# Order of the input projections beside the differential attention of a two-layer hybrid encoder

## The chip, the cores and the metric

The kernel runs on one core of a Trainium2 chip. The metric is the device time of one execution in microseconds (us), the median of several runs. The core's engines work side by side, each through its own instructions in a fixed order: PE (TensorE: matmuls and transposes), DVE (VectorE), ACT (ScalarE), POOL (GpSimd) and SP (SyncE, which here issues nearly all transfers). An instruction that has to wait holds up everything behind it on its engine.

## The reference

Two layers work on 2048 tokens of width 1024. Each projects the normalized input to 3584 columns, which four groups of heads share: A (dense attention with normalized queries and keys), B (a window of 128 to each side), C (a two-dimensional neighbourhood with a bias table), and D (differential attention: two softmaxes of all keys, one subtracted from the other). Each group's output is multiplied by its gate, then comes an output projection and the residual. The core, cut:

```python
for l in range(DEPTH):
    h = _rmsnorm(x, norm_g[l])
    z = jnp.einsum('bsd,de->bse', h, w_in[l])
    (q_a, k_a, v_a, g_a, q_b, k_b, v_b, g_b,
     q_c, k_c, v_c, g_c, q_d, k_d, v_d, g_d) = jnp.split(z, offs, axis=-1)
    q_a = _axial_rope(_rmsnorm(q_a.reshape(...), qn_a[l]), row, col)
    k_a = _axial_rope(_rmsnorm(k_a.reshape(...), kn_a[l]), row, col)
    o_a = _dense_blocked(q_a, k_a, v_a, sc_hd)
    q_b, k_b = _rope(q_b, t), _rope(k_b, t)
    o_b = _window_sink(q_b, k_b, v_b, sink_b[l], sc_hd)
    o_c = _neighbourhood(q_c, k_c, v_c, rpb_c[l], sc_hd)
    q_d, k_d = _rope(q_d, t), _rope(k_d, t)
    o_d = _diff_blocked(q_d, k_d, v_d, lam, DIFF_DIM ** -0.5)
    o_d = _rmsnorm(o_d, subln_d[l]) * (1.0 - lam_init)
    mix = jnp.concatenate([o_a * silu(g_a), o_b * silu(g_b), o_c * silu(g_c), o_d * silu(g_d)], -1)
    x = x + jnp.einsum('bsm,md->bsd', mix, w_out[l])
return _rmsnorm(x, final_g)
```

## The kernel before

The 2048 tokens are 16 tiles of 128. A layer has four stages. First the columns of D are projected for all tiles. Then comes the D phase: D's attention, in 32 units (one tile and one group of keys each), and beside it, as filler for PE, the projections of A, B and C. Then the attention of A, B and C, and last the output projection.

A unit of D makes scores on PE (S, L497, 16 of 128 x 512), takes them from PSUM with their maxima on DVE (L498), exponentiates on ACT (L505), subtracts the second softmax from the first on DVE (L724), transposes on PE (PTp, L514), copies back on ACT (L475), multiplies with the values on PE (O, L521), and finishes with a norm: DVE's L594, L595 and L597, POOL's L114 and L545, and PE's transpose L550 (fin).

The filler is a generator (`filler`) that `drive` advances by some steps at each slot of D's work. It works through `plan`: ten chunks of 256 columns for tiles 0 to 7, then the same ten for tiles 8 to 15. A tile of a chunk is 24 matmuls (z, L320, L322, L324: two parts of the input, two of the weight, eight blocks of rows), and then the chunk's post-processing:

- `q_chunk` (A's or B's queries): ACT copies; for A the squares (L737), DVE's sum (L739) and POOL's power (L114) and weight (L758); then a rotation of POOL multiplications (L334, L340 or L342) and an addition (L761, tile qs). One or two tiles later `q_store` transposes on PE (qT, L767), splits on ACT and DVE (L770, L771, tile qt, two buffers) and stores (L773).
- `kv_chunk` (keys and values of A or B): an ACT copy (zkv), the rotation on POOL for half as many columns, stores (L780, L789).
- `ck_chunk` and `cv_chunk` (C's keys, C's values): one ACT copy (zv, L828 for the values) and stores.
- `cq_chunk` (C's queries): an ACT copy (L803); later `qc_store` transposes (qT, L811), splits (L819, L820) into the tile qc, which has one buffer for two tiles of tokens, and stores it (L823).
- `g_chunk` (gates): an ACT copy (L794), a tanh (L347), DVE's product (L348, tile gs, two buffers) and a store (L797).

During the last tile of a chunk the next chunk's eight weights are loaded (wst, L307) and split by POOL (L313) and DVE (L314). Four of the first chunk's weights are loaded ahead, in the projection of D (tile wb, on ACT). As the seventh chunk (i == 6) starts, `build_rep` writes C's bias table to DRAM from one buffer (rbuf): a load (L122), POOL copies (L126, L138) and memsets (L134), and six stores (L131, L139), where each L134 after the first waits for the landing of the store before it.

The program order is only the starting point: a scheduler puts each engine's instructions of the D phase into an order of its own, the same order then holds on the chip. The stage of A, B and C keeps PE's order as written.

Of the kernel before, what the change touches and what calls it, by code (L numbers as in the profile page):

```python
# [39 lines left out]
OFF_A, OFF_B, OFF_C, OFF_D = 0, 768, 1536, 2560  # L40
# [33 lines left out]
def trunk_kernel(ctx, tc, x, norm_g, w_in, w_out, qn_a, kn_a, sink_b, rpb_c, lam_q1, lam_k1, lam_q2, lam_k2,  # L74
# [184 lines left out]
    for l in range(depth):  # L259
# [44 lines left out]
        def load_w(wp, st, k, c0, w, act=False, s=None, wt=None):  # L304
            if s is None:
                s = st.tile([128, w], F32, tag="st", name="wst")
            nc.sync.dma_start(out=s, in_=w_in[l, k * 128:(k + 1) * 128, c0:c0 + w])  # L307
            if wt is None:
                wt = wp.tile([128, 2, w], F32R, tag="w", name="wt")
            if act:  # L310
                A.activation(wt[:, 0, :], s, ACTF.Copy, scale=g8[:, k:k + 1])
            else:
                G.tensor_scalar(wt[:, 0, :], s, g8[:, k:k + 1], 0.0, op0=ALU.mult, op1=ALU.add)  # L313
            V.scalar_tensor_tensor(wt[:, 1, :], s, g8[:, k:k + 1], wt[:, 0, :].bitcast(F32),  # L314
                                   op0=ALU.mult, op1=ALU.subtract)
            return wt

        def in_proj_k(z, h, wk, k):
            kc = slice(k * 128, (k + 1) * 128)
            PE.matmul(z, lhsT=h[:, 0, kc], rhs=wk[:, 0, :], start=(k == 0), stop=False)  # L320
            yield
            PE.matmul(z, lhsT=h[:, 0, kc], rhs=wk[:, 1, :], start=False, stop=False)  # L322
            yield
            PE.matmul(z, lhsT=h[:, 1, kc], rhs=wk[:, 0, :], start=False, stop=(k == KD - 1))  # L324
# [28 lines left out]
        with tc.tile_pool(name="wd", bufs=16, reuse_waits="tile") as wp, tc.tile_pool(name="st", bufs=3, reuse_waits="tile") as st:  # L353
# [23 lines left out]
            def x_tile(t):  # L377
                xt = xtp.tile([128, D], F32R if l else F32, tag="x", name="xt")
                nc.sync.dma_start(out=xt.bitcast(F32) if l else xt, in_=xres[t])
                h = make_ht(l, t, xt, big if t < HALF else xh, tps, zp)  # L380
                if t < HALF:
                    ht[l, t] = h
                else:
                    spill_ht(l, t, h)
                return h
# [6 lines left out]
            def d_post(t, z1, z2):  # L392
                rs = rstd[l][:, t:t + 1]
                zq = zp.tile([128, 384], F32, tag="zq", name="zq")
                A.activation(zq, z1, ACTF.Copy, scale=rs)
                zg = zp.tile([128, 256], F32, tag="zg", name="zg")
                V.tensor_scalar(vd[:, t, :], z2[:, 0:128], rs, 0.0, op0=ALU.mult, op1=ALU.add)
                A.activation(zg, z2[:, 128:384], ACTF.Copy, scale=rs)
                gs = zp.tile([128, 2, 128], F32, tag="gs", name="gs")
                gate(zp, zg, gs.rearrange("p a b -> p (a b)"))  # L400
                G.tensor_tensor(gs.rearrange("p a (b d) -> p (a b) d", d=64), gs.rearrange("p a (b d) -> p (a b) d", d=64),
                                bc(sub, 1, 4), op=ALU.mult)
                nc.sync.dma_start(out=gd_d[t], in_=gs)
                cos, sin = load_rope(zp, t, 256, 32)
                r1, r2 = rope_parts(zp, zq.rearrange("p (h w) -> p h w", h=12), 12, 32, 1, cos, sin)
                qk = zp.tile([128, 12, 32], F32, tag="qk", name="qk")
                G.tensor_tensor(qk, r1, r2, op=ALU.add)
                sp = zp.tile([128, 4, 4, 32], F32R, tag="sp", name="sp")
                kb = bc(qk[:, 8:12, :], 2, 2)
                spf = sp.bitcast(F32)  # L410
                A.copy(sp[:, :, 0:2, :], kb)
                V.tensor_tensor(sp[:, :, 2:4, :], kb, spf[:, :, 0:2, :], op=ALU.subtract)
                return qk, sp

            def d_stack(t, qk, sp):
                ts = slice(t * 128, (t + 1) * 128)
                p = tps.tile([128, 512], F32, tag="t", name="qT")
                for i in range(2):
                    PE.transpose(p[:, i * 128:(i + 1) * 128], qk[:, 4 * i:4 * i + 4, :].rearrange("p a b -> p (a b)"), idn)
                qt = zp.tile([128, 2, 2, 128], F32R, tag="qt", name="qt")  # L420
                p2 = p[:, 0:256].rearrange("p (k q) -> p k q", k=2)
                A.copy(qt[:, :, 0, :], p2)
                V.tensor_tensor(qt[:, :, 1, :], p2, qt[:, :, 0, :].bitcast(F32), op=ALU.subtract)
                for m in range(4):
                    nc.sync.dma_start(out=qd_d[t][:, :, :, m, :].rearrange("k a d q -> d (k a) q"),
                                      in_=qt[m * 32:(m + 1) * 32, :, :, :].bitcast(F32).rearrange("p k a q -> p (k a) q"))
                p = tps.tile([128, 512], F32, tag="t", name="kT")
                for i in range(4):
                    transpose_raw(p[:, i * 128:(i + 1) * 128], sp[:, i, :, :].rearrange("p a b -> p (a b)"))
                for c in range(2):  # L430
                    V.tensor_copy(kd0[c][:, ts], p[:, c * 128:(c + 1) * 128])
                k1 = zp.tile([128, 256], F32R, tag="k1", name="k1")
                A.copy(k1, p[:, 256:512])
                nc.sync.dma_start(out=kd_d[0][:, :, ts], in_=k1.bitcast(F32).rearrange("p (a b) -> p a b", a=2))

            prev = None
            wpre = []
            for t in range(NT):
                h = hs.pop(t)
                if t == WPT:  # L440
                    wb = big.tile([128, 4, 2, 256], F32R, tag="b", name="wb")
                    for k in range(4):
                        s = st.tile([128, 384], F32, tag="st", name="wst")
                        wpre.append(load_w(wp, st, k, OFF_A, 256, True, s[:, 0:256], wb[:, k]))
                if t + 1 < NT:
                    hs[t + 1] = x_tile(t + 1)
                zs = []
                for c in range(2):
                    z = zps.tile([128, 384], F32, tag="z", name="z")
                    for k in range(KD):  # L450
                        for _ in in_proj_k(z, h, ws[c][k], k):
                            pass
                    zs.append(z)
                cur = d_post(t, *zs)
                if prev is not None:
                    d_stack(*prev)
                prev = (t, *cur)
# [5 lines left out]
        with tc.tile_pool(name="sm", bufs=6, reuse_waits="tile") as sm, \  # L463
# [264 lines left out]
            if True:  # L728
                ph2 = ExitStack()
                st = ph2.enter_context(tc.tile_pool(name="st2", bufs=5, reuse_waits="tile"))  # L730
                wp = ph2.enter_context(tc.tile_pool(name="w2", bufs=10, reuse_waits="tile"))
# [106 lines left out]
                ab = []  # L838
                for g, off in (("A", OFF_A), ("B", OFF_B)):
                    ab += [(g, off, q_chunk), (g, off + 256, kv_chunk), (g, off + 512, g_chunk)]  # L840
                cc = [("C", OFF_C, cq_chunk), ("C", OFF_C + 256, ck_chunk), ("C", OFF_C + 512, cv_chunk), ("C", OFF_C + 768, g_chunk)]
                order = [ab[0], cc[1], ab[1], cc[2], ab[3], cc[0], ab[4], ab[2], ab[5], cc[3]]
                plan = [(c, range(h * HALF, h * HALF + HALF)) for h in range(2) for c in order]

                pend_all = []
# [378 lines left out]
```

## Time and profile before

| | |
|---|---|
| median of three runs | 3577.78 us (3574.85 to 3580.77) |
| the profiled execution | 3572.38 us |
| its span, first to last instruction | 3570.6 us |
| mean granted clock of PE | 0.989 |
| filler of layer 0 (first to last matmul of A, B and C) | about 180 to 1027 us |
| filler of layer 1 | about 1946 to 2795 us |
| transfers | 387.47 MB, mean 109 GB/s |

The profile's page gives each engine's busy time, the chain of work that ended last, and groups of instructions by source line (L320 is line 320), with the idle time before them and what ended it. "out<-in" are the program's names of tiles. The view by stretches gives, for stretches of time, each engine's busy time with its instructions in brackets and PE's granted clock as a share of full speed. In the view in order of time, square brackets hold the idle time of the engine just before an instruction, and what ended it.

### The profile page before, as it was taken

What the parts mean: (1) busy time and instruction counts of PE and PEld (TensorE: products, weight loads), DVE (VectorE), ACT (ScalarE), POOL (GpSimd) and SP (SyncE); (2) the same over time, 40 slices, a digit from 0 to 9 for tenths busy, and PEclk for the clock granted to TensorE, in tenths of its full rate; (3) what the DMA queues carried; (4) which work ended last, traced back from release to release, by engine and by line L of the source; (5) the groups of instructions that cost most, each with busy time, mean ns of one, the idle gap of its engine ahead of it and who ended that gap; (6) DMA issues with size and microseconds to landing.
All of it is one profiled execution on the core that took longest, in us unless ns stands there. A gap on an engine that the chain in (4) does not pass through costs nothing.

```text
span 3570.6 us, 71576 instructions
## 1 busy us (share of the span) xinstructions
PE 3432.0 (96%) x25232; PEld 2964.9 (83%) x25232; DVE 2491.9 (70%) x7827; ACT 2109.9 (59%) x3963; POOL 963.4 (27%) x1604
## 2 busy tenths in 40 slices
PE   8989999999989999999999999999999899899999
PEld 8979889898967777878899888988888678678787
DVE  4387877878878887773234877787778688777733
ACT  4455656556667877771144555665566678777711
POOL 4455432552210001001044553345421000010000
PEclk9999999999999999999999999999999999999999
DMA  4532235323232345335445323252322333543243
GB/s 147 186 107 87 79 80 168 93 83 88 68 101 80 89 115 138 90 101 177 143 137 178 89 79 89 77 177 84 88 79 62 103 85 84 137 115 98 90 159 112
DMA packets 355777, 387.47 MB, mean 109 GB/s; under 512 B 59802, under 2 KB 298586, under 8 KB 350298
## 3 DMA queue, kind: packets, MB, share of 16 engines
q1 hardware_dynamic: 351098, 367.17, 34.8%
q10 hardware_dynamic: 4320, 15.73, 1.3%
q8 instruction: 199, 3.26, 0.4%
q14 instruction: 160, 1.31, 0.1%
HBM read 258.83 MB, written 123.91 MB: 107 GB/s over the span
## 4 chain that ended last, share of the span: by engine, by line
PE 78%; DVE 9%; DMA 4%; ACT 3%; POOL 3%; issue 2%; SPq 1%; DVEq 0%; POOLq 0%; ACTq 0%
PE O L521 11%; PE S L497 10%; PE PTp L514 10%; PE y L218 10%; PE z L320 9%; PE z L324 9%; PE z L322 9%; DVE P L498 4%; PE Obc L540 2%; PE PTp L532 2%; PE Sc L1044 1%; ACT P L505 1%; DMA wst<-in_w_in_dram 1%; DVE wt L314 1%; DVE P L724 1%
## 5 line engine op out<-in xcount | busy, mean ns | idle before, releaser
L498 DVE TENSOR_SCALAR_CACHE_REDUCE P<-S 128x512 f32<-128x512 f32 x1536 | 1025.4, 686 | 260.3 <-PE S L497 205.2
L320 PE MATMUL z<-wt,ht 128*128 128x256 f32 (+1 forms) x3008 | 892.7, 298 | 16.8 <-POOL wt L313 5.5
L322 PE MATMUL z<-wt,ht 128*128 128x256 f32 (+1 forms) x3008 | 887.0, 295 | 0.5 <-DVE wt L314 0.2
L324 PE MATMUL z<-wt,ht 128*128 128x256 f32 (+1 forms) x3008 | 883.1, 294 | 0.0
L514 PE MATMUL PTp<-idr,P 128*128 128x128 f32 x4096 | 630.7, 277 | 36.5 <-ACT P L475 18.2
L475 ACT COPY P<-PTp 128x512 f32<-128x512 f32 x896 | 513.3, 585 | 252.1 <-PE PTp L514 246.8
L505 ACT ACTIVATE P<-P,nm 128x2048 f32<-128x2048 f32 x256 | 514.1, 2008 | 156.6 <-DVE jk L504 153.9
L514 PEld LDWEIGHTS PTp<-idr,P 128*128 128x128 f32 x4096 | 492.2, 143 | 135.8 <-ACT P L475 34.2
L320 PEld LDWEIGHTS z<-wt,ht 128*128 128x128 f32 x3008 | 569.6, 190 | 37.7 <-POOL wt L313 7.3
L322 PEld LDWEIGHTS z<-wt,ht 128*128 128x128 f32 x3008 | 570.7, 190 | 12.5 <-DVE wt L314 2.2
L324 PEld LDWEIGHTS z<-wt,ht 128*128 128x128 f32 x3008 | 570.3, 190 | 9.2 <-issue 1.5
L497 PE MATMUL S<-kA,q 128*128 128x512 f32 x1024 | 361.9, 436 | 0.1
L218 PE MATMUL y<-wot,ms 128*128 128x512 f32 x1440 | 330.8, 392 | 0.0
L218 PEld LDWEIGHTS y<-wot,ms 128*128 128x128 f32 x1440 | 270.8, 188 | 59.7
L545 POOL TENSOR_TENSOR gg<-gt,rzh 128x128 f32<-128x128 f32 x192 | 76.7, 400 | 886.7 <-DVE rzh L606 324.5
L313 POOL TENSOR_SCALAR wt<-wst,g 128x256 fp32r<-128x256 f32 (+1 forms) x336 | 221.0, 669 | 333.3 <-PE z L324 222.1
L724 DVE SCALAR_TENSOR_TENSOR P<-P,cf,P 128x2048 f32<-128x2048 f32 x128 | 307.3, 2401 | 2.2
L505 ACT ACTIVATE P<-P,nm,rr_a 128x2048 f32<-128x2048 f32 x128 | 268.7, 2099 | 62.2 <-DVE jk L504 59.6
L521 PE MATMUL O<-P,vd 128*64 128x256 f32 x2048 | 238.5, 384 | 7.3 <-ACT P L475 7.3
L521 PE MATMUL O<-P,vA 128*64 128x256 f32 x2048 | 235.1, 382 | 0.0
L497 PE MATMUL S<-kd,qd 128*128 128x512 f32 x512 | 209.9, 428 | 9.2 <-DVE P L498 7.6
L497 PE MATMUL S<-kdt,qd 128*128 128x512 f32 x512 | 210.1, 436 | 8.4 <-DVE P L498 5.5
(195 smaller groups left out, 5103.0 us busy)
## 6 DMA issues: line engine op xcount, KB each, us to landing
wst<-in_w_in_dram SPq DMA_DIRECT2D x320, 128.0 KB
qd<-qd SPq DMA_DIRECT2D x128, 128.0 KB
htd<-ht SPq DMA_DIRECT2D x16, 1024.0 KB
ht<-htd SPq DMA_DIRECT2D x16, 1024.0 KB
q<-qsA SPq DMA_DIRECT2D x128, 128.0 KB
q<-qsB SPq DMA_DIRECT2D x64, 256.0 KB
q<-qc SPq DMA_DIRECT2D x64, 256.0 KB
mload<-mx ACTq DMA_DIRECT2D x30, 512.0 KB
```

The lines of the kernel that those rows point to most:

```text
L218: PE.matmul(ys[c], lhsT=ms[:, a, kc], rhs=wts[k][:, b, c * 512:(c + 1) * 512], start=(k == 0 and i == 0), stop=(k == KD - 1 and i == 2))
L313: G.tensor_scalar(wt[:, 0, :], s, g8[:, k:k + 1], 0.0, op0=ALU.mult, op1=ALU.add)
L320: PE.matmul(z, lhsT=h[:, 0, kc], rhs=wk[:, 0, :], start=(k == 0), stop=False)
L322: PE.matmul(z, lhsT=h[:, 0, kc], rhs=wk[:, 1, :], start=False, stop=False)
L324: PE.matmul(z, lhsT=h[:, 1, kc], rhs=wk[:, 0, :], start=False, stop=(k == KD - 1))
L475: A.copy(dst, src)
L497: PE.matmul(s, lhsT=q, rhs=k_ap[:, c:c + 512], start=(i == 0), stop=(i == len(q_list) - 1))
L498: V.tensor_scalar(p[:, c:c + 512], s, 1.0, None, op0=ALU.mult, op1=ALU.max, accum_out=mx[:, j:j + 1])
L505: A.activation(p, p, ACTF.Exp, bias=nm, scale=scale, accum_out=zacc)
L514: PE.transpose(tp[:, (h * 2 + a) * 128:(h * 2 + a + 1) * 128], p[:, h, j * 128:(j + 1) * 128], idn)
L521: PE.matmul(u["o"][a * 64:(a + 1) * 64, 0:256], lhsT=u["v"](0, j), rhs=u["p"][:, :, j * 128:(j + 1) * 128], start=(n < 2), stop=(n >= NT - 2))
L724: V.scalar_tensor_tensor(p0, p1, cf, p0, op0=ALU.mult, op1=ALU.add)
```

## The change

The list of the ten chunks is put in another order, and the weights that are loaded ahead are those of the new first chunk. Before: A queries, C keys, A keys and values, C values, B queries, C queries, B keys and values, A gate, B gate, C gate. After: C keys, A queries, C values, A keys and values, C queries, B queries, A gate, B keys and values, B gate, C gate.

```diff
@@ -441,7 +441,7 @@
                     for k in range(4):
                         s = st.tile([128, 384], F32, tag="st", name="wst")
-                        wpre.append(load_w(wp, st, k, OFF_A, 256, True, s[:, 0:256], wb[:, k]))
+                        wpre.append(load_w(wp, st, k, OFF_C + 256, 256, True, s[:, 0:256], wb[:, k]))
@@ -839,7 +839,7 @@
                 for g, off in (("A", OFF_A), ("B", OFF_B)):
                     ab += [(g, off, q_chunk), (g, off + 256, kv_chunk), (g, off + 512, g_chunk)]
                 cc = [("C", OFF_C, cq_chunk), ("C", OFF_C + 256, ck_chunk), ("C", OFF_C + 512, cv_chunk), ("C", OFF_C + 768, g_chunk)]
-                order = [ab[0], cc[1], ab[1], cc[2], ab[3], cc[0], ab[4], ab[2], ab[5], cc[3]]
+                order = [cc[1], ab[0], cc[2], ab[1], cc[0], ab[3], ab[2], ab[4], ab[5], cc[3]]
                 plan = [(c, range(h * HALF, h * HALF + HALF)) for h in range(2) for c in order]
```

What the scheduler makes of it can be seen on single engines. POOL at the opening of the filler in layer 0, before (wt are weights, gs D's gate of the stage ahead, zq, r, ars and qs the steps of A's queries):

```order
L313 TENSOR_SCALAR wt<-wst,g_95 128x256 x3
L401 TENSOR_TENSOR gs<-gs,sub 128x256
L313 TENSOR_SCALAR wt<-wst,g_95 128x256 x4
L758 TENSOR_TENSOR zq<-zq,qkn 128x256
L313 TENSOR_SCALAR wt<-wst,g_95 128x256
L758 TENSOR_TENSOR zq<-zq,qkn 128x256
L313 TENSOR_SCALAR wt<-wst,g_95 128x256
L334 TENSOR_TENSOR r_2408<-zq,rope 128x256
L342 TENSOR_TENSOR r_2409<-zq,rope 128x8x16 x2
L313 TENSOR_SCALAR wt<-wst,g_95 128x256
L114 TENSOR_TENSOR ars<-ame,epst 128x4
L761 TENSOR_TENSOR qs<-r_2408,r_2409 128x256
```

And after:

```order
L313 TENSOR_SCALAR wt<-wst,g_95 128x256 x3
L401 TENSOR_TENSOR gs<-gs,sub 128x256
L313 TENSOR_SCALAR wt<-wst,g_95 128x256 x7
L275 TENSOR_SCALAR sub<-sub 128x64
L313 TENSOR_SCALAR wt<-wst,g_95 128x256 x4
L758 TENSOR_TENSOR zq<-zq,qkn 128x256
L334 TENSOR_TENSOR r_2915<-zq,rope 128x256
L342 TENSOR_TENSOR r_2916<-zq,rope 128x8x16 x2
L761 TENSOR_TENSOR qs<-r_2915,r_2916 128x256
```

The queries of A moved behind all weights of the first two chunks; ahead of them POOL has almost nothing else. On PE, the first two chunks hold 53 scores, 72 transposes of P and 16 transposes of queries before, and 51, 68 and 12 after; in the new first chunk alone there are 20 scores and 4 transposes of P, in the second 31 and 64.

SP, the queue of transfers, at the bias table in layer 0, before (rep is the table, qc C's queries, vsB and ksB B's values and keys, qd a unit's queries of D):

```order
L131 DMA rep_6260<-rbuf 60x24x40
L131 DMA rep_6260<-rbuf 60x25x40
L139 DMA rep_6260<-rbuf 60x4x40
L307 DMA wst<-in_w_in_dram 128x256
L823 DMA qc_2_218<-qc 128x1x512 x2
L780 DMA vsB_181<-zkv 128x128
L328 DMA rope<-in_rope_dram 128x128
L789 DMA ksB_0_172<-ks 128x128
L705 DMA qd<-qd_11_114 64x512
L139 DMA rep_6260<-rbuf 60x4x40
```

And after (qsB is B's queries, gsA A's gate):

```order
L131 DMA rep_6261<-rbuf 60x24x40
L131 DMA rep_6261<-rbuf 60x25x40
L139 DMA rep_6261<-rbuf 60x4x40
L307 DMA wst<-in_w_in_dram 128x256 x2
L328 DMA rope<-in_rope_dram 128x128
L139 DMA rep_6261<-rbuf 60x4x40
L307 DMA wst<-in_w_in_dram 128x256
L773 DMA qsB_6_158<-qt 128x1x256 x2
L797 DMA gsA_0_182<-gs 128x256
L139 DMA rep_6261<-rbuf 60x4x40
L773 DMA qsB_7_159<-qt 128x1x256 x2
L797 DMA gsA_1_183<-gs 128x256
```

The store of C's queries no longer stands among the table's writes; the last two stores of B's queries and the first stores of A's gate do.

DVE near the end of the D phase in layer 0, behind the projections' last matmuls, before (s, dme and drs are steps of a unit's norm, rz the reciprocals, cf and P the subtraction of the softmaxes):

```order
L112 TENSOR_SCALAR dme<-s_13799 128x2
L498 TENSOR_SCALAR P,mx<-S 128x512 x2
L504 TENSOR_SCALAR jk,nm<-mx 128x4
L720 RECIPROCAL rz<-zt 128x2
L721 COPY rz_13744<-rz 128x1
L723 SCALAR_TENSOR_TENSOR cf<-zt,nlam_93,rz 128x1
L724 SCALAR_TENSOR_TENSOR P<-P_13746,cf,P 128x2048
L597 TENSOR_TENSOR drs<-drs,rz_12959 128x2
```

And after:

```order
L112 TENSOR_SCALAR dme<-s_13769 128x2
L498 TENSOR_SCALAR P_13716,mx<-S 128x512
L498 TENSOR_SCALAR P,mx<-S 128x512 x2
L504 TENSOR_SCALAR jk,nm<-mx 128x4
L597 TENSOR_TENSOR drs<-drs,rz_12954 128x2
L498 TENSOR_SCALAR P,mx<-S 128x512 x2
L348 SCALAR_TENSOR_TENSOR gs<-th,zg 128x256
L553 TENSOR_TENSOR mix<-fin,os 128x128
```

L597, on which POOL's L545 and then PE's L550 wait, moved from behind the large L724 to ahead of it. Behind the last matmul of the projections PE has 28 scores of D left before, and 26 after. Layer 1 has the same order at the three places but for single rows.

## The prediction

> **What bounds the kernel now.** I read the page first: the busy shares and the chain that ended last.
>
> ```profile
> span 3570.6 us, 71576 instructions
> PE 3432.0 (96%) x25232; PEld 2964.9 (83%) x25232; DVE 2491.9 (70%) x7827; ACT 2109.9 (59%) x3963; POOL 963.4 (27%) x1604
> PE 78%; DVE 9%; DMA 4%; ACT 3%; POOL 3%; issue 2%; SPq 1%; DVEq 0%; POOLq 0%; ACTq 0%
> ```
>
> PE is busy 96% of the span and is 78% of the chain. The change alters no instruction's size and adds none, so it can win or lose only what PE does not do: the stops, and the slow clock behind a stop. The profiled execution took 3572.38 us around this span; the three timed runs have a median of 3577.78. I sum against 3572.38 and carry the difference of 5.4 over to the median at the end.
>
> Next, PE's view of waits. Three of its rows belong to places that the change touches:
>
> ```profile
> PE qT L767 <- POOL qs L761: 11.0, 4, 5.2
> PE fin L550 <- POOL gg L545: 8.0, 3, 3.8
> PE qT L811 <- DVE qc L820: 7.1, 2, 4.9
> ```
>
> Then the busy time by stretches. The first two rows are the opening chunk (A's queries, first eight tiles) of layer 0 and of layer 1; the next is the same chunk for tiles 8 to 15, its twin. The short ones follow single stops, the last is the end of D's units in layer 0.
>
> ```profile
> core 0: us, PE busy (x) PEld busy (x) DVE busy (x) ACT busy (x) POOL busy (x), PEclk, DMA share, GB/s
> 179.70:228.10 48.40, 41.12 (x266) 36.30 (x265) 41.81 (x126) 25.99 (x44) 38.80 (x54) 0.89 0.43 117
> 1945.60:1998.50 52.90, 41.21 (x267) 36.09 (x267) 43.47 (x130) 25.90 (x43) 39.97 (x54) 0.90 0.38 104
> 601.80:649.10 47.30, 46.05 (x349) 39.04 (x348) 41.18 (x135) 28.81 (x54) 36.09 (x51) 1.00 0.42 129
> 201.68:205.09 3.41, 3.41 (x18) 3.41 (x17) 2.78 (x10) 0.26 (x1) 3.24 (x7) 0.50 0.34 82
> 461.10:464.51 3.41, 3.13 (x14) 3.02 (x15) 3.41 (x5) 0.87 (x3) 1.65 (x9) 0.50 0.06 11
> 2229.20:2232.61 3.41, 3.41 (x19) 3.41 (x18) 3.33 (x10) 0.31 (x1) 1.65 (x7) 0.50 0.09 16
> 1034.54:1041.37 6.83, 3.56 (x14) 3.17 (x15) 5.68 (x15) 3.11 (x4) 0.40 (x1) 0.50 1.07 240
> 1027.20:1069.70 42.50, 30.03 (x164) 19.56 (x163) 32.66 (x105) 26.45 (x38) 4.51 (x6) 0.87 0.59 161
> ```
>
> The opening chunk needs 48.4 and 52.9 us for 266 matmuls; the twin does 349 in 47.3. PE stands 7.28 and 11.69 us in it (length less busy), in the twin 1.25. And behind a stop there is a window of 3.41 us at clock 0.50, which costs PE half of it, 1.7 us.
>
> **Term 1, the opening.** PE's order of time at the opening of both layers, and POOL's groups in the opening chunk of layer 0:
>
> ```profile
> 201.09 0.44 PE L767 MATMUL qT<-idr,qs 128*128 128x128 f32 x2 [3.81 <-POOL qs L761]
> 1968.61 0.69 PE L767 MATMUL qT<-idr,qs 128*128 128x128 f32 x2 [5.16 <-POOL qs L761]
> ```
>
> ```profile
> L761 POOL TENSOR_TENSOR qs<-r,r 128x256 f32<-128x256 f32 x7 | 8.9, 1277 | 0.1
> L313 POOL TENSOR_SCALAR wt<-wst,g 128x256 fp32r<-128x256 f32 x11 | 7.1, 653 | 11.2 <-DMA wst<-in_w_in_dram 10.6 <-PE z L324 0.5
> L342 POOL TENSOR_TENSOR r<-zq,rope 128x128 f32<-128x128 f32 x14 | 6.4, 474 | 0.0
> L114 POOL TENSOR_TENSOR ars<-ame,epst 128x4 f32<-128x4 f32 x6 | 6.1, 1022 | 0.1
> L758 POOL TENSOR_TENSOR zq<-zq,qkn 128x256 f32<-128x256 f32 x7 | 5.5, 792 | 0.1
> L334 POOL TENSOR_TENSOR r<-zq,rope 128x256 f32<-128x256 f32 x7 | 5.2, 738 | 0.2
> ```
>
> A tile of A's queries costs POOL 1.28 + 2 x 0.47 + 1.02 + 0.79 + 0.74 = 4.8 us, eight of them 38.2, the next chunk's eight weights 5.2: 43.4 us, while D has little for PE yet. POOL sets the pace, and PE stops at the first transpose. With C's keys in front, POOL has weights alone there (a tile's post-processing is one ACT copy and a store), and A's queries come second, when two units of D stand between them. That is the twin's situation. The stops of 3.81 and 5.16 us go, and a half-clock window behind each: 8.97 + 2 x 1.7 = 12.4. The opening's other stops, on DVE and on the first weights, stay. The bounds are 0, if A's chunk stops PE again one place later, and 12.4. I take **11**, nearest to the twin, as the new second chunk holds more of D than the twin (64 transposes of P against 46).
>
> **Term 2, the bias table.** The writes of C's bias table (L131, L139) are issued as the seventh chunk begins, B's keys and values now, A's gate then. On SP, ACT, PE, and POOL at its end:
>
> ```profile
> 448.06 1.92 SPq L131 DMA_DIRECT2D rep<-rbuf  x2
> 450.08 2.14 SPq L139 DMA_DIRECT2D rep<-rbuf  x1
> 453.64 1.63 SPq L823 DMA_DIRECT2D qc<-qc  x2
> 458.19 0.55 SPq L139 DMA_DIRECT2D rep<-rbuf  x1
> ```
>
> ```profile
> 458.26 0.27 ACT L819 CAST qc<-qT 128x128 fp32r<-128x128 f32 x1 [9.23 <-DMA qc<-qc]
> ```
>
> ```profile
> 461.38 0.66 PE L811 MATMUL qT<-idr,qs 128*128 128x128 f32 x2 [4.91 <-DVE qc L820]
> 2227.86 0.41 PE L811 MATMUL qT<-idr,qs 128*128 128x128 f32 x2 [2.24 <-DVE qc L820]
> ```
>
> ```profile
> 463.06 0.23 POOL L134 MEMSET rbuf<- 60x160 f32 x1 [1.69 <-DMA rep<-rbuf]
> ```
>
> The store of C's queries (L823) sits on SP behind the table's writes. Its tile qc has one buffer, so ACT waits 9.23 us for the landing with all its other work behind it, and PE stops 4.91 and 2.24 us. In the new order C's queries are the fifth chunk, and behind the table's writes stand stores of B's queries and of A's gate, whose tiles have two buffers. Gone: 4.91 + 2.24 and two windows of 1.7, 10.6 us. New: the third tile of the gate, on DVE, waits for the first one's store, which is behind the second L139, 8.1 us after the first; two tiles take 2/8 of a chunk, 11.8 us by the twin, so little is left. Bounds 0 and the whole run of writes, 15.0 us from 448.06 to 463.06. I take 2 per layer: **6.6** gained.
>
> **Term 3, the end of D.**
>
> ```profile
> 1034.85 2.35 DVE L724 SCALAR_TENSOR_TENSOR P<-P,cf,P 128x2048 f32<-128x2048 f32 x1
> 1037.12 0.15 DVE L597 TENSOR_TENSOR drs<-drs,rz 128x2 f32<-128x2 f32 x1
> ```
>
> ```profile
> 1037.81 0.47 PE L550 MATMUL fin<-idr,gg 128*128 128x128 f32 x1 [3.79 <-POOL gg L545]
> ```
>
> ```profile
> L498 DVE TENSOR_SCALAR_CACHE_REDUCE P<-S 128x512 f32<-128x512 f32 x1536 | 1025.4, 686 | 260.3 <-PE S L497 205.2
> ```
>
> Once the projections are used up, PE is busy 30.03 of 42.5 us; DVE and ACT are the pace. The small L597 stands behind the large L724, and PE waits 3.79 us for the transpose that needs it. In the new order L597 stands ahead of that L724, and two fewer scores are left for this stretch. If the stop were PE's own loss, 3.79 and a window of 6.83 at 0.50, 7.2 per layer, would go; if DVE's chain is all, two scores of 0.69. Bounds 0 and 14.4; I take the scores, **2.8** for both layers.
>
> Elsewhere the new pairs (A's queries before C's values, C's queries before B's) have the same neighbours in mirrored order, and I put them at nothing: POOL's and DVE's work there lies beside PE's. Without that cover each new stop costs what the listed ones do, 2 to 5 us and a window. Sum: 11 + 6.6 + 2.8 = 20.4. 3572.38 - 20.4 = 3552.0, on the median **3557.4**.
>
> One rule changes the size alone: the Trainium skill, "TensorE: Matmul & The Clock Gate", section "Why this matters for your kernels", lets the clock fall behind gaps of more than about 3 us. The row differs: the stop of 2.24 us is followed by 0.50 too, so I count the window; by the rule the sum is 18.7.
>
> **The rivals.**
>
> - POOL stays the bound. DVE's L724 reads and writes SBUF while POOL works, and POOL stretches beside it:
>
> ```profile
> 632.50 2.77 DVE L724 SCALAR_TENSOR_TENSOR P<-P,cf,P 128x2048 f32<-128x2048 f32 x1
> ```
>
> ```profile
> 633.20 2.67 POOL L334 TENSOR_TENSOR r<-zq,rope 128x256 f32<-128x256 f32 x1
> ```
>
> L334 took 2.67 instead of 0.74 us. The new second chunk has about four such L724 (two units), 43.4 + 4 x 1.9 = 51 us of POOL against some 47 for PE, and the opening gains nothing; if the gate's store also eats term 2, term 3 alone is left: **3575**. Against it: the twin's POOL is busy 36.09 of 47.30 us with such stretches in it, and PE stands 1.25. The Trainium skill, "SBUF — State Buffer", section "SBUF: two separate sides", calls the port of both engines an exclusive lock for the whole instruction; the two rows agree.
> - The full gain: 12.4 + 10.6 + 14.4 = 37.4, **3540**. For it speaks that PE is 78% of the chain; against it, DVE in term 3.
> - Slower. The gate's store hangs behind the table's writes and DVE, not ACT, stands: its scores are not taken from PSUM, so PE stops with it. At the full 15.0 us and a window of 3.4 that is 36.8 in two layers, less the 24.4 gained (11, 10.6, 2.8): **3590**. It turns to a loss from 8.8 us per layer on. Against it: two buffers, and the 11.8 us of two tiles.
> - Nothing changes, since PE is fed by D at these places anyway: 3578. Against it, the twin.
>
> **How the numbers follow.** About 0.2%, 7.2 us, is what a measurement of this kernel can tell from no change. Forecast 0.53 (3557, between 3548 and 3567), full gain 0.17, POOL or nothing 0.18, slower 0.12. Faster 0.70, same 0.18, slower 0.12. The range goes from 3540 to 3576, which leaves out the slow case and a little beyond the full gain.
>
> **What would show it.** Term 1: no stop of over 2 us on POOL's qs in the first two chunks, and the two together near 83 us, 92.5 now in layer 0. Term 2: ACT's wait for qc under 2 us, none of DVE for the gate's store over 3. Term 3: PE's stop at L550 under 1 us. Wrong, if PE has stops of over 3 us at the second chunk or at the seventh, or if PE's idle time falls and the span does not.

## The result, and the profile after

| | before | after |
|---|---|---|
| median | 3579.07 us (4 runs) | 3554.59 us (4 runs, 3550.76 to 3557.08) |
| ratio, 95% interval | | 0.9933, 0.9922 to 0.9945 |
| span of the profiled execution | 3570.6 us | 3555.4 us |
| mean granted clock of PE, profiled | 0.989 | 0.992 (0.992 to 0.996 in the four runs) |

The change gains 24.5 us by the medians; 20.4 were predicted (3557.4 us, measured 3554.59). The two profiles differ by 15.2 us only: the profiled execution of before was a quick one (3572.38 us against a median of 3579.07), and that of after is the longest of its four (3557.08).

The page of after, its span and the busy time of each engine:

```profile
span 3555.4 us, 71573 instructions
PE 3423.0 (96%) x25232; PEld 2955.6 (83%) x25232; DVE 2489.5 (70%) x7827; ACT 2110.3 (59%) x3963; POOL 939.7 (26%) x1604
```

DVE and ACT did the same work in the same time. PE was busy 9 us less for the same 25232 instructions: that fits the clock, since there are fewer stretches at clock 0.50 (see below). POOL was busy 23.7 us less (963.4 before) for the same 1604 instructions; where that comes from was not taken apart. The view by stretches (start and end, length, then busy time and instructions of PE, its weight load, DVE, ACT and POOL, then PE's clock, the busy share of the DMA engines and their GB/s) for the first two chunks, then for chunks 4 to 6 (numbered from 0), of both layers, before:

```profile
179.70:272.20 92.50, 83.50 (x596) 73.66 (x596) 76.13 (x229) 48.82 (x81) 49.62 (x71) 0.94 0.37 105
1945.60:2041.20 95.60, 83.19 (x595) 73.10 (x595) 76.41 (x230) 48.83 (x80) 50.12 (x70) 0.95 0.35 101
347.30:491.80 144.50, 137.37 (x1060) 120.90 (x1059) 109.88 (x331) 82.79 (x147) 63.91 (x117) 0.99 0.32 84
2116.40:2258.60 142.20, 137.50 (x1060) 121.06 (x1059) 109.92 (x331) 83.01 (x147) 65.92 (x117) 0.99 0.33 86
```

And after, with the end of D's units in both layers as the last two rows (42.3 and 41.4 us before, from the same place on):

```profile
181.60:266.50 84.90, 79.01 (x584) 71.02 (x583) 69.41 (x207) 46.53 (x77) 45.51 (x63) 0.96 0.35 102
1941.00:2024.90 83.90, 77.68 (x584) 69.72 (x583) 69.46 (x208) 46.47 (x77) 45.41 (x61) 0.98 0.35 102
344.60:491.70 147.10, 140.41 (x1071) 121.86 (x1070) 113.40 (x349) 88.27 (x158) 53.88 (x108) 0.99 0.31 83
2103.20:2247.60 144.40, 138.48 (x1070) 120.45 (x1070) 113.68 (x350) 88.51 (x158) 53.82 (x108) 1.00 0.32 84
1028.00:1065.80 37.80, 29.16 (x159) 18.41 (x160) 31.15 (x99) 25.88 (x38) 4.69 (x6) 0.91 0.60 175
2784.10:2821.20 37.10, 28.13 (x158) 18.15 (x158) 30.97 (x99) 25.77 (x38) 4.69 (x6) 0.91 0.63 178
```

The opening got 7.6 and 11.7 us shorter. Chunks 4 to 6, where the second term was to be won, got 2.6 and 2.2 us longer, partly because 11 more of PE's instructions fall into them. Lengths mislead here, since the scheduler shifts work of D from one stretch to the next. What PE loses in a stretch is better: its idle time (all gaps of over 0.15 us between its rows), plus half of the time at clock 0.50. Length less this loss, summed over the D phases of both layers, is 1679 to 1688 us in all fourteen kernels of this study; so the loss tells where time came from, within some us. For the D phase, in us, layer 0 / layer 1:

| stretch | before | after | first two chunks exchanged, tiles 0 to 7 | two buffers for qc | after, old opening |
|---|---|---|---|---|---|
| chunks 0 to 1 | 13.6 / 17.0 | 8.7 / 7.3 | 8.7 / 10.2 | 17.2 / 16.9 | 13.4 / 15.9 |
| 2 to 3 | 1.4 / 1.4 | 2.3 / 2.9 | 3.7 / 4.3 | 1.5 / 1.4 | 0.3 / 0.3 |
| 4 to 6 | 8.4 / 6.0 | 7.7 / 5.5 | 7.3 / 10.6 | 1.8 / 2.2 | 1.7 / 2.9 |
| 7 to 9 | 0 / 0 | 0 / 0 | 0 / 0 | 0 / 0 | 0.5 / 0 |
| 10 to 13 | 3.1 / 3.6 | 3.3 / 4.6 | 6.9 / 6.8 | 3.2 / 2.4 | 3.0 / 2.9 |
| 14 to 16 | 3.1 / 4.9 | 5.6 / 5.0 | 3.1 / 4.9 | 2.1 / 2.3 | 3.6 / 1.6 |
| 17 to 19 | 0.2 / 0.2 | 0.7 / 0.7 | 0.2 / 0.2 | 0 / 0 | 0.2 / 0.2 |
| end of D | 17.1 / 16.0 | 11.1 / 11.7 | 14.8 / 16.9 | 18.0 / 20.0 | 15.5 / 14.6 |
| sum | 47.0 / 49.1 | 39.4 / 37.7 | 44.7 / 53.9 | 43.8 / 45.1 | 38.2 / 38.4 |

From before to after: opening 14.6 us less, chunks 4 to 6 1.2 less, end of D 10.3 less, and 7.2 more in the stretches where the prediction put nothing (2 to 3, 10 to 19). Of the 19 us in all, 8.1 are idle time and 10.8 are half of 21.6 us less at clock 0.50. The measure is a little generous: idle time that falls into a stretch at clock 0.50 is counted one and a half times, which makes 5.6 us too many before and 0.2 after. By length the two D phases got 16.8 us shorter.

The view of waits shows what took the place of the stops. Of before, two rows that were not shown yet:

```profile
PE S L497 <- DVE P L498: 13.1, 26, 3.1
...
PE PTp L514 <- DVE P L724: 5.2, 2, 2.8
```

And after (engine, line, what it waited for: total, times, longest); the rows "qT <- POOL qs L761", "fin <- POOL gg L545" and "qT <- DVE qc L820" of before are gone:

```profile
PE S L497 <- DVE P L498: 18.1, 31, 2.1
...
PE PTp L514 <- DVE P L724: 13.2, 14, 2.8
...
ACT qc L819 <- DMA qc<-qc: 10.6, 8, 2.6
...
DVE gs L348 <- DMA gc<-gs: 4.9, 2, 2.6
...
PE z L320 <- ACT qs L803: 4.7, 4, 1.2
```

In chunks 4 to 6 of layer 0, PE's order of time has one long stop before (the 4.91 us on qc) and these after:

```profile
369.02 0.39 PE L320 MATMUL z<-wt,ht 128*128 128x256 f32 x1 [1.18 <-ACT qs L803]
...
392.19 0.50 PE L497 MATMUL S<-kd,qd 128*128 128x512 f32 x1 [0.67 <-DVE P L498]
...
408.67 0.44 PE L514 MATMUL PTp<-idr,P 128*128 128x128 f32 x2 [1.15 <-DVE P L724]
...
431.37 0.44 PE L514 MATMUL PTp<-idr,P 128*128 128x128 f32 x2 [0.45 <-DVE P L724]
...
449.16 0.50 PE L497 MATMUL S<-kd,qd 128*128 128x512 f32 x1 [1.17 <-DVE P L498]
...
458.09 1.72 PE L497 MATMUL S<-kd,qd 128*128 128x512 f32 x3 [0.65 <-DVE P L498]
```

Together 5.27 us, as much as the stop they replace; layer 1 has five of the same. Five of the six end with DVE, in D's own chain, and the first with ACT's copy of C's queries. Why DVE is late differs from stop to stop. Ahead of the second and the third it splits C's queries (L820). Ahead of the other three it had itself stood idle shortly before, for POOL's weights of the next chunk or for ACT's exponentials of D:

```profile
428.45 0.17 DVE L720 RECIPROCAL rz<-zt 128x2 f32<-128x2 f32 x1 [2.22 <-ACT P L505]
...
447.81 0.69 DVE L314 SCALAR_TENSOR_TENSOR wt<-wst,g,wt 128x256 fp32r<-128x256 f32 x1 [1.92 <-POOL wt L313]
...
456.95 0.17 DVE L720 RECIPROCAL rz<-zt 128x2 f32<-128x2 f32 x1 [1.83 <-ACT P L505]
```

The store of A's gate, which the prediction watched, does not stop DVE in the seventh chunk at all. The row "gs <- DMA gc<-gs" above is C's gate in the tenth chunk (at 592.4 and 2348.1 us).

At the end of D the small L597 stands ahead of the L724 now (DVE's order of time), and PE's transpose L550 does not stop; the next thing late there is a copy of P by ACT (PE's):

```profile
1031.45 0.15 DVE L597 TENSOR_TENSOR drs<-drs,rz 128x2 f32<-128x2 f32 x1
...
1034.21 2.35 DVE L724 SCALAR_TENSOR_TENSOR P<-P,cf,P 128x2048 f32<-128x2048 f32 x1
```

```profile
1032.14 0.33 PE L550 MATMUL fin<-idr,gg 128*128 128x128 f32 x1
...
1036.65 1.56 PE L514 MATMUL PTp<-idr,P 128*128 128x128 f32 x8 [1.81 <-ACT P L475]
```

### The profile page after: what moved, and what is told of

The parts are those of the page before. It is cut to its first block, busy times and chain, and to the rows that moved or that the text cites. A ratio compares the mean times of both kernels' runs of the same rounds, so it can differ in the third digit from the quotient of the medians.

```text
span 3555.4 us, 71573 instructions
## 1 busy us (share of the span) xinstructions
PE 3423.0 (96%) x25232; PEld 2955.6 (83%) x25232; DVE 2489.5 (70%) x7827; ACT 2110.3 (59%) x3963; POOL 939.7 (26%) x1604
## 4 chain that ended last, share of the span: by engine, by line
PE 69%; DVE 9%; ACT 4%; DMA 2%; issue 2%; POOL 2%; SPq 0%; ACTq 0%; DVEq 0%; POOLq 0%
PE y L218 10%; PE O L521 10%; PE S L497 9%; PE PTp L514 9%; PE z L320 7%; PE z L322 7%; PE z L324 7%; DVE P L498 4%; ACT P L505 2%; PE Obc L540 2%; PE PTp L532 2%; DVE P L724 2%; PE Sc L1044 1%; DMA mx<-mix 1%; ACT P L475 1%
## 5 line engine op out<-in xcount | busy, mean ns | idle before, releaser
L545 POOL TENSOR_TENSOR gg<-gt,rzh 128x128 f32<-128x128 f32 x192 | 76.9, 402 | 885.0 <-DVE rzh L606 315.5
L724 DVE SCALAR_TENSOR_TENSOR P<-P,cf,P 128x2048 f32<-128x2048 f32 x128 | 306.5, 2395 | 2.7
L313 POOL TENSOR_SCALAR wt<-wst,g 128x256 fp32r<-128x256 f32 (+1 forms) x336 | 203.5, 617 | 332.6 <-PE z L324 226.9
L314 DVE SCALAR_TENSOR_TENSOR wt<-wst,g,wt 128x256 fp32r<-128x256 f32 (+1 forms) x344 | 193.1, 588 | 44.5 <-POOL wt L313 41.0
```

The costliest lines, as they stand in the source:

```text
L724: V.scalar_tensor_tensor(p0, p1, cf, p0, op0=ALU.mult, op1=ALU.add)
```

## Experiments

The medians below are set against runs of the kernel before on the same chip (3577 to 3579 us).

**1. The opening alone.** Kernel before, with the first two chunks exchanged for tiles 0 to 7 (and C's keys loaded ahead).

```diff
+first = [cc[1], ab[0], ab[1], cc[2], ab[3], cc[0], ab[4], ab[2], ab[5], cc[3]]
-plan = [... for h in range(2) for c in order]
+plan = [... for h in range(2) for c in (first if h == 0 else order)]
```

> The kernel before, with only the first two chunks of tiles 0 to 7 exchanged (C's keys, then A's queries); the second half and the end of D keep their order. If POOL's backlog at the opening is a loss of its own, the first two chunks take some 7.6 and 11.7 us less in the two layers, as in the changed kernel, at most 3 us each of it comes back in the next two chunks, and the whole is 11 to 16 us faster (about 3563 to 3568). Rival: D's units set the pace of the opening, the chunks only borrow work from the ones behind: then chunks 0 to 3 together are less than 2 us shorter per layer and the whole is within 4 us of before.

Measured: 3577.42 us, ratio 1.0002 (0.9993 to 1.0012). The opening did get 7.5 and 9.1 us shorter, and lost 11.7 us less (14.6 in after); but chunks 2 to 3 lose 5.2 more, chunks 4 to 6 of layer 1 4.6 more, and chunks 10 to 13, whose list is unchanged, 7.0 more. The rows of these chunks, before and then here:

```profile
601.80:766.70 164.90, 161.31 (x1258) 143.70 (x1258) 129.87 (x404) 94.92 (x163) 89.72 (x148) 1.00 0.33 97
2368.30:2533.30 165.00, 161.09 (x1259) 143.70 (x1258) 129.70 (x404) 94.65 (x163) 90.12 (x148) 1.00 0.33 96
```

```profile
596.30:766.60 170.30, 163.16 (x1279) 146.18 (x1278) 133.01 (x417) 100.74 (x171) 90.68 (x148) 1.00 0.32 95
2367.60:2537.30 169.70, 164.36 (x1278) 147.72 (x1277) 133.35 (x414) 100.79 (x170) 91.56 (x149) 0.99 0.32 94
```

PE has some 20 instructions more there and stands 7.1 and 5.3 us instead of 3.6 and 3.9. So D is at another place when the second half begins.

**2. The middle alone.** Kernel before, chunks 4 to 7 of tiles 0 to 7 in the new order.

```diff
+first = [ab[0], cc[1], ab[1], cc[2], cc[0], ab[3], ab[2], ab[4], ab[5], cc[3]]
```

> The kernel before, with chunks five to eight of tiles 0 to 7 as in the change (C's queries, B's queries, A's gate, B's keys and values); the opening and the second half as before. The prediction's term 2: the stop on qc (4.91 and 2.24 us) goes and the stretch from the fifth to the seventh chunk is 3 us shorter per layer. Rival, from the changed kernel's trace: B's queries behind C's queries make new stops on DVE (scores not yet taken from PSUM, the subtraction L724) of 4 to 6 us in the sixth chunk, and the stretch is no shorter, within 2 us of before per layer. The end of D gets another order too, which is read by itself.

Measured: 3586.23 us, ratio 1.0027 (1.0015 to 1.0039): slower. Chunks 4 to 6 are 7.7 and 5.5 us shorter and lose 6.6 us less, but the projections then run out ahead of D. 43 scores instead of 28 are left for the end, where PE is busy only three quarters of the time:

```profile
1012.40:1070.50 58.10, 45.13 (x243) 29.23 (x243) 48.50 (x158) 39.28 (x57) 5.79 (x8) 0.88 0.43 122
2786.10:2845.70 59.60, 46.19 (x245) 28.69 (x243) 48.72 (x158) 39.50 (x57) 5.80 (x8) 0.91 0.43 120
```

The longer end is not what makes it slower, though. In lost time it costs 3.1 us more than before, and run 8 below has as long an end and is faster than before. The larger part, 6.3 us, comes in chunks 10 to 16, whose list is unchanged.

**3. The table two chunks later.** Kernel before, with the call of `build_rep` moved.

```diff
-if i == 6:
+if i == 8:
```

> The kernel before, with the bias table written at the ninth chunk (B's gate) in place of the seventh; the chunks' order is that of before. If the stop on qc comes from the table's writes on SP, ACT's wait for qc in layer 0 falls from 9.23 us to under 2, PE's stops of 4.91 and 2.24 us at L811 vanish, nothing takes their place, and the kernel is 6 to 11 us faster (3568 to 3573). Rival: the one buffer of qc stops ACT wherever C's queries are followed by anything: then the stop stays, and the time is that of before within 3 us.

Measured: 3576.4 us, 0.9999 (0.999 to 1.0007). A miss: the scheduler put the table's writes where they had been (first row, SP), PE's order is the same to the row, and ACT still waits (second row).

```profile
448.61 1.91 SPq L131 DMA_DIRECT2D rep<-rbuf  x2
```

```profile
457.77 0.27 ACT L819 CAST qc<-qT 128x128 fp32r<-128x128 f32 x1 [8.47 <-DMA qc<-qc]
```

What it gives is a measure of chance: for one order on PE, two profiles lost 47.0 / 49.1 and 47.9 / 45.1 us. A difference of up to 4 us in one layer of one profile says nothing.

**4. The transpose at the end later on PE.** Kernel before, in the fourth unit from the end.

```diff
+units[-4]["f2"] = 5
```

> The kernel before, with PE's last transpose of one unit of D (the one whose L550 stops PE for 3.79 us behind the projections' end) put two slots later; DVE's order in that stretch stays as it was. If the stop is PE's own loss, the stretch from the projections' last matmul to A's first scores shrinks from 42.3 and 41.4 us to about 38 in each layer, as in the changed kernel, and the whole is some 8 us faster (3571). If DVE's and ACT's chain sets it, as the prediction took it, PE's stop goes, the stretch stays within 1 us, and the time is that of before.

Measured: 3574.54 us, 0.9992 (0.9983 to 1.0001). The end got 2.0 and 1.1 us shorter, but the stop is still there (PE's order of time, layer 0; 3.79 in layer 1 too), so the run doesn't tell what the stop is worth:

```profile
1040.99 0.48 PE L550 MATMUL fin<-idr,gg 128*128 128x128 f32 x1 [3.79 <-POOL gg L545]
```

**5 and 6. The change in one half of the tiles.** The new list for tiles 0 to 7 alone, then for tiles 8 to 15 alone.

```diff
+plan = [... for h in range(2) for c in (new if h == 0 else old)]
...
+plan = [... for h in range(2) for c in (old if h == 0 else new)]
```

> The new list for tiles 0 to 7 alone (with the new first weights); tiles 8 to 15 keep the old list. Measure: what PE loses in a stretch, its idle time plus half of the time at clock 0.50. Between the two profiles at hand it fell by 4.7 and 8.7 us (layer 0, layer 1) in chunks 0 to 9, by 2.8 and 2.7 in chunks 10 to 19 and the end of D. Theory 'the parts add': this kernel keeps the first pair, 13 us, ratio about 0.9963, the opening near 84 us per layer, the end of D near 42. Rival 'only together' (as where the first two chunks alone were exchanged, and the 11 us of the opening came back in chunks 2 to 3 and 10 to 13): ratio 0.999 to 1.001, chunks 10 to 13 lose 3 to 4 us per layer more than before. Rival 'the second half makes it': 1.000, with nothing lost in chunks 10 to 13.

> The old list for tiles 0 to 7, the new one for tiles 8 to 15. 'The parts add': opening as before (92 to 96 us), the end of D near 37.5 instead of 42 us; 5.5 us less in all, ratio about 0.9985, and this kernel and the one with the other half together give the 24 us of the whole change. 'Only together': 0.9995 to 1.001. 'The second half makes it': 0.995 or less.

Measured: first half 3557.9 us, 0.9954 (0.994 to 0.9967); second half 3577.86 us, 1.0002 (0.9993 to 1.0012). Two thirds of the gain come with the first half, nothing with the second alone; the last third needs both, or is chance (the intervals of the first half and of the whole change overlap). With the first half new, the end of D is 37.6 us long although its own list is the old one: so the end does not hang on the list of the second half alone. That it is set by where D stands by then is the likely reading.

**7. Only the first two chunks, in both halves.**

```diff
+order = [cc[1], ab[0], ab[1], cc[2], ab[3], cc[0], ab[4], ab[2], ab[5], cc[3]]
```

> Only the first two chunks exchanged, in both halves (C's keys, then A's queries), all else in the old order. With the exchange in the first half alone the opening gave 11.7 us of lost time back, and chunks 10 to 13, where A's queries then met a unit of D at another place, lost 7.0 more. If that meeting was the cause, chunks 10 to 13 are back near 3 us lost, and the ratio is about 0.997. Rival: what comes back does not hang on the place of A's queries in the second half, then it is 0.999 to 1.001 as with the first half alone. Rival: C's queries ahead of B's are what the gain needs, then also 1.000, with chunks 4 to 6 as before and the end of D near 42 us.

Measured: 3572.39 us, 0.9984 (0.9975 to 0.9993). Chunks 10 to 13 are back at 3.1 and 3.4 us lost, as the first theory had it, though the ratio that it gave was 0.997; the end of D still loses 17.8 and 16.7.

**8. The wait for qc alone.** Kernel before; the tile qc half as large, with two buffers, each tile of tokens stored for itself.

```diff
-if t % 2 == 0:
-    qcp[0] = zp.tile([128, 2, 2, 2, 4, 32], F32R, tag="qc", name="qc", bufs=1)
+qt = zp.tile([128, 2, 2, 2, 2, 32], F32R, tag="qc", name="qc")
...
-if t % 2:
-    for hh in range(2):
-        nc.sync.dma_start(...)
+for hh in range(2):
+    for x in range(2):
+        nc.sync.dma_start(...)
```

> Kernel before, with C's queries stored tile by tile: the tile qc is half as large and has two buffers, with eight small stores for two tiles of tokens instead of two, so that ACT need not wait for the store behind the table's writes. This is the second term of the prediction alone. As predicted: PE's stops of 4.91 and 2.24 us at L811 and their half clock go, 6.6 to 10.6 us, ratio 0.997 to 0.998, chunks 4 to 6 at 140 and 138 us instead of 144.5 and 142.2. Rival: PE stops at the next thing that is late there, D's scores behind DVE, and the ratio is 0.9995 to 1.0005; then the stop on qc is gone and the wait S <- P L498 is longer by as much. Rival: the eight stores hold up SP, 1.001 and more.

Measured: 3560.38 us, 0.9954 (0.9942 to 0.9967), more than any of the theories gave it. ACT's wait for the store, 21.3 us in all before, is this:

```profile
ACT qc L817 <- DMA qc<-qc: 1.5, 2, 0.8
```

PE's longest stop at the transposes of C's queries is 0.4 us, and chunks 4 to 6 are down by 6.7 and 3.6 us for the same instructions; the end of D got longer, as more of D is left for it:

```profile
347.70:485.50 137.80, 135.57 (x1060) 119.19 (x1058) 109.78 (x331) 83.00 (x146) 62.62 (x118) 1.00 0.35 91
2110.20:2248.80 138.60, 135.91 (x1059) 119.13 (x1058) 109.15 (x327) 82.75 (x146) 64.02 (x118) 1.00 0.34 89
1005.70:1064.20 58.50, 46.33 (x243) 28.99 (x243) 48.04 (x152) 38.52 (x57) 5.82 (x8) 0.88 0.44 121
```

In lost time the profile shows 7.2 us less, and its span is 11.5 us shorter; as the profile of before was a quick execution, the 17 us of the medians are the better figure. Chunks 4 to 6 lose 10.4 us less; where the rest of the 17 comes from is not shown. The run also stores in four times as many transfers, and the scheduler's order changes with it, so it is not the wait alone that differs.

**9 to 11. The change with one part added or undone.** After with the two buffers; after with the old first two chunks in tiles 0 to 7; after with B's queries ahead of C's queries, and B's keys and values ahead of A's gate, in both halves.

```diff
+first = [ab[0], cc[1], cc[2], ab[1], cc[0], ab[3], ab[2], ab[4], ab[5], cc[3]]
...
+order = [cc[1], ab[0], cc[2], ab[1], ab[3], cc[0], ab[4], ab[2], ab[5], cc[3]]
```

> Kernel after, with C's queries stored tile by tile from two half-size buffers, as in the run that did this alone in the kernel before (0.9954). In after, ACT still waits 10.6 us in 8 for the store of qc and 16.6 us in 15 for DVE's L820. Theory 'each removes stops of its own': the waits for the store go, chunks 4 to 6 fall from 147.1 and 144.4 us to about 142, ratio to before 0.990 to 0.992. Rival 'one cause': the change gained by taking C's queries away from the table's writes, which is what the two buffers do too, so both together give no more than one: 0.993 to 0.995. Rival: the eight small stores and the more scores left at the end (31 instead of 26) eat it: 0.995 and more.

> Kernel after, with the first two chunks of tiles 0 to 7 back in the old order (A's queries, then C's keys, and A's weights ahead); all else new. Theory 'the opening's stops are lost time': the first two chunks are back at 92 and 95 us with POOL's stops of 4 to 5 us, 9 to 15 us slower than after, ratio to before 0.996 to 0.998. Rival 'the opening comes back later anyway' (as in the first run, 1.0002): D is further ahead, so the rest is as much faster; ratio 0.993 to 0.994 as in after.

> Kernel after, with B's queries again before C's queries and B's keys and values before A's gate, in both halves; the first four chunks stay new. If C's queries away from the table's writes are what the first half gains, chunks 4 to 6 show ACT's wait of 8 to 9 us for the store of qc and PE's stop at L811 again, and the ratio is 0.996 to 0.998, near that of the two exchanged chunks alone (0.9984). If C's values before A's keys and values matter, it stays below 0.9950, as in after, with waits for the store of qc under 4 us.

Measured: 3555.81 us, 0.9942 (0.9929 to 0.9954); 3558.37 us, 0.9946 (0.9933 to 0.9958); 3561.02 us, 0.9948 (0.9934 to 0.9962). Each interval overlaps that of the change. The two buffers bring nothing on top of it, as "one cause" had it, but not by its path. Chunks 4 to 6 lose 7.7 us less with them here too (5.5 instead of 13.2), and chunks 10 to 13 and the end lose 9.2 more; so the change alone had left most of that loss in place. Without the new opening, 13.3 us more are lost in chunks 0 to 1 and 7.3 more at the end, but 13.2 less in chunks 2 to 6 and 8.4 less in chunks 10 to 19: the sum is the same. With the old opening, then, the new middle does what term 2 promised: chunks 4 to 6 lose 4.6 us instead of 14.4 before. The stops that stand there in after hang on how far D has come, and not on the new neighbours alone. With the old middle, ACT waits for the store of qc again, but PE's stop at L811 does not return (1.0 us at most):

```profile
ACT qc L819 <- DMA qc<-qc: 16.0, 5, 4.4
```

**12. C's values ahead of A's keys and values alone**, in both halves of the kernel before.

```diff
+order = [ab[0], cc[1], cc[2], ab[1], ab[3], cc[0], ab[4], ab[2], ab[5], cc[3]]
```

> Kernel before with C's values ahead of A's keys and values (third and fourth chunk), in both halves, nothing else: the one exchange that was not tried alone. The prediction put it at nothing. With the first two chunks exchanged in both halves the ratio was 0.9984, with this exchange on top 0.9948. Theory 'this exchange carries the gain': 0.9955 to 0.997, with the opening as before (92 to 96 us) and the stops at L811 gone. Rival 'no exchange carries it alone': 0.999 to 1.001, with the stops at L811 of 2 to 5 us still there. If the ratio is low while the stops at L811 stay, C's store is not what it removes, and the time must be missing at the end of D (42 us) or in chunks 10 to 16.

Measured: 3571.03 us, 0.9982 (0.9973 to 0.9991), between the two. The stop at L811 is down to 0.9 us, yet chunks 4 to 6 lose as much as before (8.3 and 7.5), by stops for D's scores instead, of 2.60 us in both layers and this one:

```profile
467.29 1.11 PE L497 MATMUL S<-kd,qd 128*128 128x512 f32 x2 [2.25 <-DVE P L498]
```

This exchange deserves more than its place at the end of the list. Alone it gains 6 us, as much as the new opening in both halves (run 7). The run with the old middle is these two together: 18 us, 0.9948, with an interval that touches neither of theirs. The new middle on top of them (0.9933) lies within the uncertainty. So the opening and this exchange give most of the change, and the prediction put this one at nothing. Every changed order here with a ratio below 0.997 has it in the first half; the opening and the middle together without it were not run. Where its time goes is not shown: the profiles of run 7 and of the run with the old middle lose the same (89.5 and 89.6 us), yet their D phases differ by 7.8 us in length (1776.6 and 1768.8), which the measure of loss does not explain.

No run was faster than after.

## Why the prediction was right, and where its steps were not

Sign and size were right: 24.5 us by the medians, 20 to 28 by the interval, for 20.4. The terms were not, and their errors cancelled; that the sum fits so well is luck in good part.

- **Term 1, the opening (11 us).** The mechanism was right: no wait on POOL's qs is left, the first two chunks take 84.9 and 83.9 us (83 was named), and 14.6 us less are lost there. What failed is the step that put the new neighbours elsewhere at nothing. In tiles 0 to 7 alone the exchange gains nothing (1.0002), in both halves 6 us, in both on top of C's values some 12 (0.9982 to 0.9948); undone in tiles 0 to 7 of after it costs 3.8 us, within the uncertainty. That the opening is won and the other chunks can pay it back is shown; what it is worth hangs on their order.
- **The pairs put at nothing.** This step failed in both directions. The mirrored pairs were put at nothing, since POOL's and DVE's work there lies beside PE's. But C's values ahead of A's keys and values gain 6 us alone and some 13 on top of the new opening (0.9984 to 0.9948), while chunks 2 to 3 and 10 to 19 of after lose 7.2 us more than before.
- **Term 2, the bias table (6.6 us).** The stop on qc is gone, and taken away by itself it saves 10.4 us of loss in chunks 4 to 6 (14.4 before, 4.0 with two buffers), where the term counted 10.6 for the two stops and their half clock. In the change only 1.2 are saved. The failing step is the question of what is late next. The gate's store was named, and DVE never waits for it there. D's own chain through DVE and ACT was not named, and gives five of the six stops of 0.45 to 1.18 us; with the old opening most of these are absent. "ACT's wait for qc under 2 us" also failed, at 2.6: the tile still has one buffer.
- **Term 3, the end of D (2.8 us).** Mis-sized: the end got 4.5 and 4.3 us shorter (42.3 to 37.8, 41.4 to 37.1). The prediction took DVE's chain to be all, and counted two scores, 2.8 us; the loss fell by 10.3, nearer to the 14.4 of the case that it did not take. The figures say that the stop was PE's own: idle time fell by 3.8 and 2.5 us, against a stop of 3.79, and the time at clock 0.50 by 4.5 and 3.5. As the stop stayed in run 4, this rests on the two profiles and on the run with the first half alone, where the stop is gone too and the end is 37.6 us long.
- **The rivals.** POOL did not stay the bound, nor did the gate's store cost a unit of D. The full gain of 37.4 was not reached, for what failed in term 2 and for what the opening paid back. No stop of over 3 us stands at the second chunk (2.1 at most) or the seventh.

What stays open is why the parts don't add: alone, the opening gives 0 or 6 us, C's values 6, the middle a loss of 10; together they give 24. Shown is that each order changes how far D has come at each chunk, where PE stops, and how many scores are left for the end (26 in after). Their number does not set the time: run 2 has 43 and is the slowest, run 8 has 42 and is 26 us faster. Which meeting of D with which chunk costs what was not taken apart further, so the cause of the 24 us as a whole stays open.

## What to carry to other kernels

Where a scheduler interleaves two streams, a stop that is removed is worth what is left of it over the whole phase: sum the idle time and the half-clock time of the bounding engine by stretch, and price what is late next, before counting it. Test a part both alone and undone in the finished change. Where a wait comes from a single buffer behind other stores, halving the tile to get two buffers may give most of what a new order gives: 17 us here, where the new order gave 24. And count every exchange that an order makes: the one that was put at nothing was worth as much here as the one that was counted at 11 us.

## What the hardware showed that was not expected

Whether a stop costs the clock hangs on where it falls. The windows at clock 0.50 start on a fixed grid of 3.413 us in each execution. The same stop of 2.81 us at the end of D in layer 0, ahead of the transposes behind the last L724, in PE's order of time and by stretches, before:

```profile
1069.41 0.69 PE L514 MATMUL PTp<-idr,P 128*128 128x128 f32 x2 [2.81 <-DVE P L724]
```

```profile
1065.26:1068.67 3.41, 1.34 (x14) 0.60 (x10) 2.12 (x4) 1.71 (x4) 0.00 (x0) 1.00 0.68 272
1068.67:1075.50 6.83, 6.09 (x24) 5.20 (x24) 4.28 (x14) 2.19 (x5) 1.09 (x2) 0.50 0.04 5
```

And after:

```profile
1065.61 0.44 PE L514 MATMUL PTp<-idr,P 128*128 128x128 f32 x2 [2.81 <-DVE P L724]
```

```profile
1061.12:1064.54 3.42, 1.68 (x16) 0.86 (x12) 1.79 (x4) 2.05 (x4) 0.00 (x0) 1.00 0.74 297
1064.54:1067.95 3.41, 2.34 (x14) 1.84 (x14) 2.87 (x8) 1.29 (x3) 0.00 (x0) 1.00 0.01 2
```

Before, 2.06 us of the stop lie in one window of the grid, and the next two are at half clock. After, the grid splits it into 1.73 and 1.08, and the clock stays full. Over the fourteen profiles, from the first record of the clock on (some 17 us into the span), each window at full clock in which PE stood 1.9 us or more was followed by half clock, 125 of 125; with 1.5 to 1.9 us it was 57 of 120; with 0.7 to 1.0 us 5 of 233. The Trainium skill, "TensorE: Matmul & The Clock Gate", section "What's actually happening", has a free-running window of 3413 ns, and the trace agrees; by its table the clock falls after an idle window, and here a window that is idle for little more than half does it. Stops within one window add up: in 8 of the 125 no single one was over 1.5 us. The four executions of after go with their clock: the shortest, 3550.76 us, at 0.996, the longest, 3557.08 us, at 0.992.
